# Expert weights in a mixture of experts: four gates, four ups, four downs per group, the four experts side by side

## The chip, the cores and the metric

The kernel runs on one core of a Trainium2 chip. The metric is the device time of one execution in microseconds (us); the kernel before has a median of 1077.59 us over three runs (1072.44 to 1079.12).

A core has a tensor engine (PE; its weight loads are shown as PEld), a vector engine (DVE), a scalar engine (ACT), a pool engine (POOL) and a sync engine (SP), which here issues nearly all transfers from DRAM.

## The reference

The program is a net of two blocks on 256 tokens of 1024 channels. The part that matters here is the mixture of experts at the end of the first block, with 32 experts of width 256 and two experts per token:

```python
def hier_moe(xn, w_group, b_group, w_router, b_router, w_gate, w_up, w_down):
    ...
    def per_sequence(args):
        xs, cw = args
        hg = jnp.einsum('sd,edf->sef', xs, w_gate)
        hu = jnp.einsum('sd,edf->sef', xs, w_up)
        act = jax.nn.silu(hg) * hu * cw[..., None]
        return jnp.einsum('sef,efd->sd', act, w_down)
```

The gate and up matrices of an expert are 1024 x 256, its down matrix is 256 x 1024, all float32: 1.05 MB each, 96 of them, 100.7 MB in all. The mixers, the attention and the two dense blocks around it are not touched.

## The kernel before

**Slots.** `route` gives each expert 32 slots for tokens. The experts are taken in eight groups g of four; `gather(S, g)` (line 1613) brings the tokens of a group's 4 x 32 slots, channels on partitions, into the tile `xg`, by 32 products into `pxg` and eight evacuations. An expert's 32 slots are one quarter of the array's 128 columns and one quarter of the partitions of the product's bank. If an expert has more than 32 tokens, `overflow` (line 1661) computes all; it stands behind a branch (line 1667) that all engines take ahead of group 2, and it does not run with these inputs.

**Products.** `gate_up(g, eps, p)` (line 1793) takes a list of expert pairs. For the gates, then for the ups, it goes over eight pieces j of the channels and, inside, over the experts of the list; each product has 32 slot columns as weights and 256 weight columns of the expert streaming, and goes to the expert's quarter of the bank `pgu`. For group 0 both pairs are in the list; from group 1 on `gate_up` is called once for each pair. `down(g, ...)` (line 1811) transposes the activations (`paT`, copied to `aT`), and multiplies them with the four down matrices: expert outermost, then the column half c, then the row half k, 512 columns each, into the two banks `pyd`. Each bank is scaled (`mg`, DVE), split in two parts (`mh` on ACT, `ml` on DVE), and eight products (`pacc`) add it to the token rows. In the main loop `down(g - 1)` stands between the two pairs of `gate_up(g)`. A float32 product is two records in the trace.

**Loads.** `moe_order` (line 1724) is the order of the 96 loads: gate, up, gate, up of a group's first pair, then the four downs of the group before, then the second pair. `moe_loads` gives each load a tile: one of the eight slots `w` (2048 columns, a ring in which load n waits for the readers of load n - 8), or, for the first 28 loads alone, idle work tiles `we` too. `moe_done` says that a weight is read, and announces the next loads. The loads for the attention behind the experts (`attn_w_in`, line 718) and for its modulation (`ada_w`, line 442) come in the same ring and on the same queue of SP, behind the last down.

**Order.** Each engine works its instructions off in a fixed order, laid out ahead of time; an instruction that waits holds up all that stand behind it on its engine.

Of the kernel before, what the change touches and what calls it, by code (L numbers as in the profile page):

```python
# [17 lines left out]
PSUM = bass.MemoryType.PSUM  # L18

T = 256  # L20
# [69 lines left out]
def shape_constants():  # L90
    """Tables that follow from the shapes alone, packed along the free axis."""
# [29 lines left out]
    # those of the first mixer, and two that are used once  # L121
# [15 lines left out]
    # mean over the last w tokens, less the token: columns t for rows s  # L137
# [15 lines left out]
class Net:  # L153
# [19 lines left out]
    # now: the tensor engine's time so far, by a coarse count of its columns and of the waits that fill() is told;  # L173
    # loaded: when the last load ends.  They only choose the order in which independent work is issued.
# [7 lines left out]
    def later(self, name, gen, lane=0):  # L182
        """lane 0: products; lane 1: products with one column, at the pace of their loads."""
        self.lanes[lane].append((name, gen))
# [15 lines left out]
    def fill(self, gap):  # L200
        """Queued work for a wait of that many microseconds."""
# [14 lines left out]
    def warm(self, n, after=None):  # L216
        """Products that nobody reads, for a wait of the tensor engine: its clock is halved after idle windows.
        They start when the columns `after` are there."""
# [8 lines left out]
    def more(self, n):  # L227
        """n steps of the second lane"""
        for _ in range(n):
            if self.lanes[1]:  # L230
                self.step(1)

    def need(self, *names):
        """Queued work up to the end of the named pieces."""
        for n in names:
            lane = next((i for i in range(2) if any(m == n for m, _ in self.lanes[i])), None)
            while n not in self.done:
                self.step(lane)

    def behind(self, *ins):  # L240
        """what is traced inside is issued behind these instructions on their engines"""
# [24 lines left out]
    def t4(self, name, dt=F32):  # L266
        """[128, 1024] work tile."""
# [14 lines left out]
    def used(self, waits=True):  # L282
        """the last slot is read by now"""
# [4 lines left out]
    def split(self, w, perm=None):  # L288
        """float32 [128, 1024] as a sum of two float32r parts; perm reorders the columns on the way."""
# [82 lines left out]
    def small_loads(self):  # L372
        """a few small loads behind a large one"""
# [22 lines left out]
    def rsqrt(self, out, v):  # L396
        """out = v ** -0.5 for a few columns, on the Pool engine."""
        return self.nc.gpsimd.tensor_tensor(out, v, self.mhalf.to_broadcast(list(v.shape)), op=ALU.pow)  # L398

    def head_rsqrt(self, sq, prep, between=None):  # L400
        """sq [128 (2 heads), 4 pairs, 256]: (prep(sum over a head))**-0.5 on every partition of the head;
        yields (bank, psum [128, 512])."""
# [11 lines left out]
    def tok_bcast(self, v, width, between=None):  # L414
        """v [128 tokens, (a, h)] -> per pair of 128-row groups, psum [128, 2, 256] with v[t, h]**-0.5 on width rows."""
# [21 lines left out]
    def ada_load(self, srcs, k):  # L437
        """rows 8 * p + k of the pieces, 2048 columns."""
# [7 lines left out]
    def ada_steps(self, which, srcs, rows, name, out, rowwise=False):  # L446
        """silu(c) @ W + b for four pieces of 512 columns: [128, 16], column j*4+q is channel chunk q of piece j;
        rows: where the biases of the first and of the second two pieces are."""
# [14 lines left out]
    def ada_half(self, half, m):  # L463
        """the first shift and scale for half of the channels: columns 4 * half.. and 8 + 4 * half.. of m."""
# [29 lines left out]
    def ada_cols(self, p, rows, name, out, rowwise=False):  # L494
        """out["m"]: channels 128 * column + partition; out["rows"]: channels 8 * partition + column"""
# [24 lines left out]
    def vector_sum(self, which, srcs):  # L520
        """silu(c) @ W for 2048 columns, on the vector engine: psum, 512 columns on each quarter of the partitions."""
# [19 lines left out]
    def ada_vector(self, which, srcs, rows, name, out):  # L541
        """as ada_steps, on the vector engine."""
# [3 lines left out]
    def gate_rows(self, l, out):  # L546
        """the gates of layer l of block 2 as rows in DRAM"""
# [23 lines left out]
    def rows_of(self, m, name):  # L571
        """m [128, 8 channel chunks] as rows on all partitions: [128, 1024]."""
# [16 lines left out]
    def combine(self, m, wname, w0, name):  # L589
        """per-channel scale w * (1 + scale); the shift is m[:, 0:8]."""  # L590
# [6 lines left out]
    def ss(self):  # L597
        """sums of squares [128 tokens, 3 parts of the channels, 2]"""
        return self.mpool.tile([128, 3, 2], F32, name="ss", tag="ss")

    def squares(self, ss, a, c, x, junk=None, first=True):
        """ss[:, c, a] = sum of squares of x [128, n]; the first half's is turned into its part of the mean."""
# [33 lines left out]
    def turn(self, xn, parts=1):  # L636
        """tokens [128, D] x 2 -> four banks [128 channels, 2 chunks x 256 tokens]."""
# [9 lines left out]
    def modulate(self, banks, scale, shift, fb=0):  # L647
        """normed rows in the channel layout, modulated: [128, 4 chunks x 256] x 2, with two float32r parts."""
# [57 lines left out]
    # Weights come as a stream of pieces in the order in which they are announced: each piece is split one ahead  # L706
    # of its use, over the borders between products too.
    def cols(self, W, c0, n, perm=None, kcs=range(8)):
        """announces columns c0..c0+n of W [1024, *] (n = 512 or 256), rows of the chunks kcs."""
# [1909 lines left out]
```

## Time and profile before

| what | us |
|---|---|
| median of three runs (lowest, highest) | 1077.59 (1072.44, 1079.12) |
| profiled execution, span from first to last instruction | 1071.7 |
| PE busy in it | 1018.5 (95%) |
| products `pgu` of the experts, first to last start | 293.2 to 535.2 |
| products `pyd`, last start | 548.7 |
| transfers, mean over the span | 265 GB/s |

The span is cut by the page into 40 slices of 26.8 us; the experts' products fill slices 11 to 20 (from 0, both included). In a row of the windows view the columns are the stretch, its length, the busy time of PE, PEld, DVE, ACT and POOL with the number of records, the granted clock of PE as a share of full speed, the busy share of the transfer engines, and GB/s. A busy PE is not a PE at its peak: records overlap, and four that run at the same time on four quarters of the array count as one busy stretch.

### The profile page before, as it was taken

Reading aid. Unit: us, or ns where it says so; the run is one execution under the profiler, and the core shown is the slowest. Engines: PE = TensorE matmul, PEld = TensorE weight load, DVE = VectorE, ACT = ScalarE, POOL = GpSimd, SP = SyncE. Lnnn points to the kernel's source line nnn. Section 1 sums busy time; section 2 is a strip of 40 time slices with the busy share of each in tenths; the row PEclk is TensorE's granted clock in tenths of the full one; section 3 lists DMA queues with packets and bytes.
Section 4 is the critical chain, followed back from the end, with each engine's and each line's share of the span. In section 5 each row is a group of like instructions: output and inputs, shape, how many; then the busy total and the mean of one; then the engine's idle time right before and its main releaser. Section 6 shows DMA issues by size and latency. Waiting matters only on the chain.

```text
span 1071.7 us, 18282 instructions
## 1 busy us (share of the span) xinstructions
PE 1018.5 (95%) x7681; PEld 771.9 (72%) x7681; DVE 558.5 (52%) x939; ACT 419.8 (39%) x685; POOL 40.7 (4%) x55
## 2 busy tenths in 40 slices
PE   5899999989998999999979999999999999999996
PEld 2587776776764544455338688999889889999995
DVE  1485645666612212102145746897878775544446
ACT  2363223252411111011036655655554557454453
POOL 1020000010100000000000001010000000000000
PEclk9999999997999999999999999999999999999999
DMA  8998856997786799989876732499998954555501
GB/s 270 312 323 328 300 198 237 364 353 266 270 343 237 272 370 392 369 340 399 343 276 209 263 114 101 156 352 373 359 331 342 322 190 158 165 195 191 196 1 40
DMA packets 88635, 284.53 MB, mean 265 GB/s; under 512 B 10526, under 2 KB 13907, under 8 KB 76519
## 3 DMA queue, kind: packets, MB, share of 16 engines
q1 hardware_dynamic: 86794, 280.31, 71.0%
q0 software_dynamic: 800, 1.57, 0.6%
q8 instruction: 61, 1.00, 0.4%
q10 hardware_dynamic: 956, 1.47, 0.4%
q14 instruction: 24, 0.19, 0.0%
HBM read 282.25 MB, written 1.07 MB: 264 GB/s over the span
## 4 chain that ended last, share of the span: by engine, by line
PE 62%; DVE 3%; ACT 1%; issue 1%; POOL 0%; POOLq 0%
PE pB L180 21%; PE pm L180 16%; PE pgu L180 8%; PE pyd L180 6%; PE pxg L180 2%; PE pacc L180 2%; PE po L180 2%; PE pgv L180 1%; PE pada L454 1%; PE pss L180 1%; PE pso L180 1%; DVE x L1428 0%; POOL rstd L398 0%; PE ppl L180 0%; DVE wl L294 0%
## 5 line engine op out<-in xcount | busy, mean ns | idle before, releaser
L294 DVE TENSOR_TENSOR wl<-w,wh 128x1024 fp32r<-128x1024 f32 x186 | 226.1, 1222 | 124.4 <-ACT wh L293 119.3
L293 ACT CAST wh<-w 128x1024 fp32r<-128x1024 f32 x186 | 194.0, 1049 | 208.2 <-PE pB L180 102.7
L180 PE MATMUL pB<-hh,wh 128*128 128x256 f32 x800 | 218.7, 289 | 2.3 <-ACT wh L293 1.5
L180 PE MATMUL pB<-hh,wl 128*128 128x256 f32 x800 | 215.3, 285 | 0.8 <-DVE wl L294 0.8
L180 PE MATMUL pB<-hl,wh 128*128 128x256 f32 x800 | 214.1, 284 | 0.8 <-DVE hl L654 0.7
L180 PEld LDWEIGHTS pB<-hh,wh 128*128 128x128 f32 x800 | 148.6, 191 | 18.2 <-issue 11.1
L180 PEld LDWEIGHTS pB<-hh,wl 128*128 128x128 f32 x800 | 147.9, 192 | 4.3 <-issue 2.3
L180 PEld LDWEIGHTS pB<-hl,wh 128*128 128x128 f32 x800 | 148.2, 192 | 1.5 <-DVE hl L654 1.2
L180 PE MATMUL pgu<-w,xg 128*32 128x256 f32 x864 | 105.6, 380 | 1.6 <-ACTq L1667 1.6
L180 PE MATMUL pm<-wh,fh 128*128 128x512 f32 (+1 forms) x262 | 101.3, 388 | 0.0
L180 PE MATMUL pm<-wl,fh 128*128 128x512 f32 (+1 forms) x262 | 100.9, 386 | 0.0
L180 PE MATMUL pm<-wh,fl 128*128 128x512 f32 (+1 forms) x262 | 100.7, 385 | 0.0
L180 PEld LDWEIGHTS pgu<-w,xg 128*32 128x32 f32 x864 | 51.9, 110 | 48.7 <-issue 7.6
L1829 DVE SCALAR_TENSOR_TENSOR mg<-pyd,slotw,g_f 128x512 f32<-128x512 f32 x16 | 12.0, 751 | 129.7 <-PE pyd L180 110.4
L534 DVE SCALAR_TENSOR_TENSOR w<-w,csil 128x1024 f32<-128x1024 f32 x56 | 70.3, 1277 | 4.3 <-DMA w<-in_ada_w_dram 4.3
L180 PE MATMUL pyd<-w,aT 128*32 128x512 f32 x208 | 62.2, 595 | 0.9 <-ACT aT L1816 0.9
L180 PEld LDWEIGHTS pm<-wh,fh 128*128 128x128 f32 x262 | 49.2, 188 | 12.2 <-ACT fsq L2231 2.5
L180 PEld LDWEIGHTS pm<-wh,fl 128*128 128x128 f32 x262 | 49.3, 188 | 9.8
L180 PEld LDWEIGHTS pm<-wl,fh 128*128 128x128 f32 x262 | 49.3, 188 | 9.6 <-DVE wl L294 0.3
L180 PEld LDWEIGHTS pyd<-w,aT 128*32 128x32 f32 x208 | 16.5, 110 | 38.6 <-issue 37.2
L1830 ACT CAST mh<-mg 128x512 fp32r<-128x512 f32 x16 | 9.7, 618 | 81.3 <-DVE mg L1829 81.3
L454 PE MATMUL pada<-w,csil 128*32 128x512 f32 x256 | 39.3, 603 | 0.0
(554 smaller groups left out, 1332.3 us busy)
## 6 DMA issues: line engine op xcount, KB each, us to landing
w<-in_mlp_w_dram SPq DMA_DIRECT2D x64, 1024.0 KB
w<-in_ada_w_dram SPq DMA_DIRECT2D x40, 1024.0 KB
w<-in_ada_w_dram SPq DMA_DIRECT2D x64, 512.0 KB
w<-in_moe_w_gate_dram SPq DMA_DIRECT2D x27, 1024.0 KB
w<-in_moe_w_up_dram SPq DMA_DIRECT2D x27, 1024.0 KB
w<-in_moe_w_down_dram SPq DMA_DIRECT2D x25, 1024.0 KB
w<-in_w_in_dram SPq DMA_DIRECT2D x12, 1024.0 KB
w<-in_attn_w_in_dram SPq DMA_DIRECT2D x9, 1024.0 KB
```

The source lines that it names most:

```text
L180: self.nc.tensor.matmul(out, lhsT, rhs, **kw)
L293: nc.scalar.copy(h, w)
L294: self.split_ins = nc.vector.tensor_sub(l, w, h)
L454: nc.tensor.matmul(acc[32 * j:32 * j + 32, :], self.csil[:, which, k:k + 1].to_broadcast([128, 32]), w[:, j * 512:(j + 1) * 512], start=(k ...
L534: nc.vector.scalar_tensor_tensor(acc[:, s], w[:, s], ck, acc[:, s], op0=ALU.mult, op1=ALU.add)
L1829: nc.vector.scalar_tensor_tensor(yg[:, s], py[c], cwg, gate[:, s], op0=ALU.mult, op1=ALU.mult)
L1830: self.down_ins = [nc.scalar.copy(yh[:, s], yg[:, s]), nc.vector.tensor_sub(yl[:, s], yg[:, s], yh[:, s])]
```

## The change

The order of the loads is by kind: the four gates of a group, its four ups, its four downs. `gate_up` is called once for each group, with four experts inside each j, and `down` of a group follows its own `gate_up`, the gather of the next group and the slot weights, and no longer stands inside the next group. In `down` the expert is the innermost loop, inside c and k. `moe_done` of the gates, and then of the ups, names four weights in place of two. The residual's products stand ahead of the last `down`. Comments and docstrings are gone, which moves line numbers by 5 to 8. Nothing is computed otherwise.

```diff
     def moe_order(self):
-        for g in range(9):
-            for ep in range(2):
-                if g < 8:
-                    for e in (4 * g + 2 * ep, 4 * g + 2 * ep + 1):
-                        yield "gate", e
-                        yield "up", e
-                if g > 0 and ep == 0:
-                    for e in range(4 * g - 4, 4 * g):
-                        yield "down", e
+        for g in range(8):
+            for kind in ("gate", "up", "down"):
+                for e in range(4 * g, 4 * g + 4):
+                    yield kind, e
...
-        def gate_up(g, eps, p):
-            es = [e for ep in eps for e in (2 * ep, 2 * ep + 1)]
+        def gate_up(g, p):
             for m, kind in enumerate(("gate", "up")):
                 for j in range(8):
-                    for e in es:
+                    for e in range(4):
...
-                self.moe_done(*((kind, 4 * g + e) for e in es))
+                self.moe_done(*((kind, 4 * g + e) for e in range(4)))
...
-            for e, k, c in ((e, k, c) for e in range(4) for c in range(2) for k in range(2)):
+            for c, k, e in ((c, k, e) for c in range(2) for k in range(2) for e in range(4)):
...
             p = self.ps("pgu")
+            gate_up(g, p)
             if g == 0:
-                gate_up(0, (0, 1), p)
                 self.overflow_flag(S)
                 gate = self.ada_gate(S["gate"], 1, "g_f")
-            else:
-                gate_up(g, (0,), p)
-                down(g - 1, *prev)
-                gate_up(g, (1,), p)
+            t = act(p)
             self.slot_weights(S, g)
-            prev = act(p), S["ot"], S["cwg"]
+            ot, cwg = S["ot"], S["cwg"]
             if g < 7:
                 self.gather(S, g + 1)
...
-        residual()
-        down(7, *prev)
+            if g == 7:
+                residual()
+            down(g, t, ot, cwg)
         return acc, fw, fw2
```

On PE, one group in the middle of the stage, before: the second pair's `pgu` and the `paT` of a group, then the first pair of the next group, then the downs, and the next pair. `pcw` are the slot weights, `pxg` the next gather.

```order
L180 MATMUL pgu<-w,xg 32x256 x32
L1814 MATMUL paT<-cs,actm 128x128 x2
L180 MATMUL pgu<-w,xg 32x256 x31
L180 MATMUL pyd<-w,aT 32x512 x16
L1642 MATMUL pcw<-cs,oh 128x128 x2
L180 MATMUL pcw<-cw,oh 128x32 x2
L180 MATMUL pacc<-mh,slotT 128x512 x2
L180 MATMUL pxg<-oh,xp 128x128 x2
```

The same place now:

```order
L180 MATMUL pgu<-w,xg 32x256 x61
L1809 MATMUL paT<-cs,actm 128x128 x2
L180 MATMUL pyd<-w,aT 32x512 x16
L180 MATMUL pacc<-mh,slotT 128x512 x2
L180 MATMUL pgu<-w,xg 32x256
L180 MATMUL pacc<-ml,slotT 128x512 x2
L180 MATMUL pacc<-mh,slotT 128x512
L180 MATMUL pacc<-ml,slotT 128x512
L180 MATMUL pacc<-mh,slotT 128x512
L180 MATMUL pacc<-ml,slotT 128x512
L1642 MATMUL pcw<-cs,oh 128x128 x2
```

The 61 rows in one piece are gates and ups of all four experts, and the downs follow the transposes at once; one product of the next group's gates has moved up between the `pacc`.

On SP, the last loads of the experts and the first behind them, before:

```order
L1763 DMA w<-in_moe_w_gate_dram 128x2048
L1763 DMA w<-in_moe_w_up_dram 128x2048
L1761 DMA w<-in_moe_w_down_dram 128x2x1024 x4
L1763 DMA w<-in_moe_w_gate_dram 128x2048
L1763 DMA w<-in_moe_w_up_dram 128x2048
L1763 DMA w<-in_moe_w_gate_dram 128x2048
L1763 DMA w<-in_moe_w_up_dram 128x2048
L1761 DMA w<-in_moe_w_down_dram 128x2x1024 x3
L1758 DMA w<-in_moe_w_down_dram 128x2x512 x2
L718 DMA w<-in_attn_w_in_dram 128x8x256
```

And now:

```order
L1758 DMA w<-in_moe_w_gate_dram 128x2048 x4
L1758 DMA w<-in_moe_w_up_dram 128x2048 x4
L1756 DMA w<-in_moe_w_down_dram 128x2x1024 x3
L1753 DMA w<-in_moe_w_down_dram 128x2x512 x2
L718 DMA w<-in_attn_w_in_dram 128x8x256
```

In the ring of eight, a down now takes the slot of a gate of its own group, the next group's gates take those of the ups, and its ups those of the downs. The loads behind the last down, and all other queues, have kept their order.

## Rows read from the trace of the kernel before

**Rows 1.** Windows view, three stretches of the experts' stage, with its column line.

```profile
core 0: us, PE busy (x) PEld busy (x) DVE busy (x) ACT busy (x) POOL busy (x), PEclk, DMA share, GB/s
406.50:440.00 33.50, 32.03 (x216) 16.01 (x214) 5.49 (x13) 4.93 (x11) 0.00 (x0) 1.00 0.92 371
440.00:474.20 34.20, 32.03 (x228) 17.44 (x226) 5.49 (x13) 5.98 (x12) 0.00 (x0) 1.00 0.89 356
505.60:549.50 43.90, 41.80 (x193) 14.93 (x190) 5.29 (x12) 2.98 (x6) 0.00 (x0) 1.00 0.94 368
```

**Rows 2.** Windows view, two stretches of ten us inside the same stage.

```profile
440.00:450.00 10.00, 10.00 (x64) 3.80 (x61) 0.00 (x0) 0.00 (x0) 0.00 (x0) 1.00 1.02 412
480.00:490.00 10.00, 10.00 (x46) 4.24 (x42) 3.12 (x5) 1.41 (x3) 0.00 (x0) 1.00 1.01 422
```

**Rows 3.** Windows view: all of group 0's gate_up; one pair; one group's downs.

```profile
293.20:300.30 7.10, 7.10 (x130) 4.13 (x130) 0.00 (x0) 2.79 (x5) 0.00 (x0) 1.00 0.57 205
307.20:314.20 7.00, 7.00 (x66) 3.63 (x65) 0.00 (x0) 1.50 (x4) 0.00 (x0) 1.00 1.01 414
410.30:418.80 8.50, 8.50 (x35) 2.33 (x32) 0.75 (x1) 0.62 (x1) 0.00 (x0) 1.00 1.02 425
```

**Rows 4.** Timeline of PE, a group's pair and downs: start, length, line, products.

```profile
403.45 6.88 PE L180 MATMUL pgu<-w,xg 128*32 128x256 f32 x61
...
410.38 8.41 PE L180 MATMUL pyd<-w,aT 128*32 128x512 f32 x31
```

**Rows 5.** Timeline of SP's queue: first gate loads of groups 6 and 7, later loads.

```profile
440.16 0.34 SPq L1763 DMA_DIRECT2D w<-in_moe_w_gate_dram  x1
...
474.33 0.34 SPq L1763 DMA_DIRECT2D w<-in_moe_w_gate_dram  x1
...
531.77 4.39 SPq L718 DMA_DIRECT2D w<-in_attn_w_in_dram  x4
541.61 6.29 SPq L442 DMA_DIRECT2D w<-in_ada_w_dram  x3
```

**Rows 6.** Timeline of PE, from group 0 to the branch ahead of group 2.

```profile
302.12 0.38 PE L1642 MATMUL pcw<-cs,oh 128*128 128x128 f32 x2
...
303.39 3.84 PE L180 MATMUL pxg<-oh,xp 128*128 128x128 f32 x32 [0.52 <-DVE oh L1617]
...
339.20 0.40 PE L180 MATMUL pgu<-w,xg 128*32 128x256 f32 x1 [1.59 <-ACTq L1667]
```

**Rows 7.** Timeline of ACT, the gathered tokens' evacuation in group 0.

```profile
307.26 1.50 ACT L1635 ACTIVATE xg<-pxg,fr,sc_f 128x128 f32<-128x128 f32 x4 [3.01 <-PE pxg L180]
```

**Rows 8.** Chain of work that ended last, in order of time, the last group.

```profile
537.09 0.42 PE paT L1814 x2
537.54 0.38 ACT aT L1816
537.96 3.66 PE pyd L180 x13
...
547.64 0.76 DVE mg L1829
548.42 0.63 ACT mh L1830
549.08 0.69 DVE ml L1830
549.77 0.67 DVE mg L1829
```

**Rows 9.** Instructions of the tile `pyd`: ns shortest, median, longest, starts.

```profile
L180 PE MATMUL pyd<-w,aT x208: 592/593/618, 324.1 to 548.7; 128*32 128x512 f32 x104
```

**Rows 10.** Line 1928 (POOL's two loads of 512 KB), time to landing.

```profile
DMA to landing us min/median/max: 4.1/5.8/7.5
```

**Rows 11.** Windows view, stretches of two us ahead of the experts' stage.

```profile
262.00:264.00 2.00, 1.61 (x4) 1.17 (x4) 2.00 (x3) 0.96 (x2) 0.00 (x0) 0.50 0.12 47
264.00:266.00 2.00, 2.00 (x6) 0.19 (x4) 1.84 (x4) 0.00 (x0) 0.00 (x0) 0.50 0.60 156
266.00:268.00 2.00, 2.00 (x10) 1.44 (x9) 0.00 (x0) 0.00 (x0) 0.00 (x0) 0.93 1.02 397
```

**Rows 12.** Windows view, a stretch of ten us behind the experts' stage.

```profile
560.00:570.00 10.00, 9.65 (x72) 7.46 (x72) 9.08 (x16) 7.63 (x15) 0.00 (x0) 1.00 0.34 115
```

More of the change, by code (lines that the diff above doesn't have):

```diff
@@ L1847, in residual @@
                             start=False, stop=False)
-        prev = None
         for g in range(8):
```

## Prediction

> **What bounds the kernel now.** I went first to the windows view of the experts' stage (293 to 549 us of the span). In its later groups PE is busy for 32.0 of 33.5 and of 34.2 us, and the transfers run at a share of 0.89 to 0.94 with 356 to 371 GB/s [rows 1]. Both look full, so the question is which of the two has air in it.
>
> PE has. Group 0 is the one group whose gates and ups already have all four experts side by side: 130 records in 7.1 us [rows 3]. One pair alone, 66 records and so half the work, takes 7.0 us [rows 3]. A column quarter of the array thus takes its own share of the time, the quarters run together, and a pair leaves half of the array idle. The downs are worse: with the expert outermost, neighbouring products share a quarter, and 32 records take 8.5 us [rows 3, 4]. Each streams twice the columns of a gate record; at the pace of group 0 (7.1 us for 32 steps of four records, 0.22 us a step), 8 steps of 0.44 us would be 3.5 us.
>
> The transfers have little. Where nothing holds them up they move 412 to 422 GB/s at a busy share of 1.01 and more [rows 2]. Over a whole group the rate is lower, because SP waits for PE to read slots. With 12 loads of 1.0486 MB per group, 417 GB/s means 2.51 us a load and 30.2 us a group, where the loads of group 7 begin 34.2 us behind those of group 6 [rows 5].
>
> So the change takes about half of PE's product time out of the stage, and the stage then runs into the transfers. The gain is what lies between 256 us and the time of the bytes, plus what the start and the end cost.
>
> **The change, step by step.** The sum goes in the profiled execution (span 1071.7 us).
>
> *Start, PE still the bound.* Up to the end of the gather for group 1 (303.39 + 3.84 = 307.2 us) nothing moves [rows 6]. Then, instead of group 1's first pair, the downs of group 0: 0.87 us from `paT` to `pyd` [rows 8], 3.5 us of products, and some 3.0 us through `mg` 0.76, `mh` 0.63, `ml` 0.69 [rows 8] and the last `pacc`: 314.6. Gate and up of group 1, 7.1 us [rows 3]: 321.7. Slot weights and gather, from 302.12 to 307.2 in group 0 and so 5.1 us [rows 6]: 326.8. ACT evacuates the gathered tokens ahead of `aT`, 1.5 us [rows 7], plus 0.87: 329.2. Downs 3.5 and the way to the last `pacc` 3.0: 335.7. Branch, 1.6 us of wait [rows 6]: 337.3. Before, PE passes the branch at 339.2 [rows 6] with the downs of group 1 still to do. Gate and up of group 2, 7.1: 344.4.
>
> In that time the loads are not late: 20 of 96 were issued before 293 us, the next eight take 20 us from the first release at 297 us, the ups of group 2 get their slots by 321.7, and its downs by 332.7 and the branch. They are through by about 341. The first loads of group 3 take the slots of group 2's ups, so they start when those are read: 344.4.
>
> *Middle, the transfers the bound.* From there on only the ring of eight is left. A down needs the slot of a gate of its own group, which is read while the ups come in; the next gates need the ups' slots, read while the downs come in. PE's work per group is 7.1 + 3.5 + 5.1 + 3.0 + 1.5 (activation) + 0.9 = 21.1 us against 30.2, and each piece (3.5 to 8 us) fits into the 10 us in which four loads come. So PE's work is hidden behind the transfers; if that cover went, a group would cost its excess over 30.2. The residual, 7 us in group 7, lies in such a wait too. Sixty loads from 344.4 take 60 x 2.51 = 150.8 us. Of the two bias tables that POOL fetches behind the branch I charge one, 512 KB, 1.3 us; the other falls into the pause before 344.4. Last byte: 496.5 us.
>
> *End.* What is late next is the last down. I have no landing time for SP's loads; POOL's of 512 KB land in 4.1 us at the shortest [rows 10], less 1.3 us of bytes 2.8 us. That is my upper bound, zero the lower; I take 2.8 since the start at 344.4 also holds an issue: 499.3. The last expert's load comes in two column halves, and c is now outermost, so its first half is done 1.3 us sooner. Left are four steps for each half. At full clock both are through at 501.6, at half clock (3.6 us each) at 505.2.
>
> PE will have waited some ten us with single products in between. This trace shows 2.4 GHz through the whole stage (1.00 in every window), but the clock at 0.50, that is 1.2 GHz, at 262 to 266 us, where only four to six products stand in two us; it rose again in the dense stretch from 266 us [rows 11]. I take 505.2. Before, the last `pyd` ends at 548.7 + 0.6 = 549.3 [rows 9]. That is 44.1 us. Behind it lie the first `pacc` and the norm; with the clock still rising I give back 1 us, between 0 and 3.
>
> *Behind the stage.* The attention's first four loads were issued at 531.8 and three more for the modulation at 541.6, ahead of the stage's end [rows 5]. Now they queue behind the last down, and the latter wait for its slots, which all come free at the end and not expert by expert. So the seven come about 10 us later against the end of the stage. The first of them, which the attention needs first, still lands with it; the rest has the stretch at a share of 0.34 as cover [rows 12]. I charge nothing; if that cover failed, up to 5 us.
>
> Sum: 1071.7 - 44.1 + 1.0 = 1028.6 us of span. The three runs lie 0.7 to 7.4 us above this span, their median 5.9, so **1034 us** beside 1077.6.
>
> **Rules that speak against it.** In the Trainium skill, "DMA: Bandwidth & Descriptors", the section "Where 436 GB/s comes from" says that from DRAM to the core's memory about 358 GB/s per core is the limit. By that a load would take 2.93 us, and the estimate would be 25 us later, some 1059. The trace does not agree: 412 to 422 GB/s over ten us [rows 2]. "TensorE: Matmul & The Clock Gate", section "HAM oscillation — how this bites in real kernels", says that products that wait for transfers in every round find the clock throttled each time; that is the last rival below, and this stage, kept busy so far, cannot show it.
>
> **The rivals.**
>
> *Downs not four wide.* No row shows 512-column products on four quarters in turn. If they stay at 8.5 us, that is 5 us more for groups 0, 1 and 2 each before the ring runs evenly, 5 at the end, and a pause of some 1 us where the ups wait for the downs' slots in the other four: 24 us, 1058. For it: 1.6 quarters at a time is what the trace has for 512 columns. Against it: the order, not the width, explains that, and `pgu` shows full overlap.
>
> *Slower transfers.* If the long windows, 356 to 371 GB/s [rows 1], are the true long-run rate and not gaps made by PE, say 365, a load costs 2.87 us, and sixty cost 22 us more: 1056. Against it, a share of only 0.89 to 0.94 in the same rows.
>
> *Handovers.* If a release reaches SP late or PE's pieces run past 8 us, because they start at 1.2 GHz, each of the three handovers in a group leaves a pause. At 1 us each over four groups: 12 us, 1046.
>
> *No gain.* The stage stays as it is, because its time is already that of the bytes, 1072 to 1079. That needs the rate of rows 1 and a late start together.
>
> *Slower than before: half clock all through.* If the clock stays at 1.2 GHz in the whole stage, the products double: 14.2 + 7.0 + 10.2 + 3.0 + 1.5 + 0.9 = 36.8 us a group, 294 for eight instead of 256, and the result is some 1115 us. It ends up slower from the point at which a group takes over 32 us, that is with two thirds of this work at half clock. For it: the dip of rows 11. Against it: PE would then have no waits left, and in the dense stretch of rows 11 the clock came back.
>
> **How the numbers follow.** The main case gets 0.72. From its bounds (landing 0 to 2.8, end at full or half clock, give-back 0 to 3, cover behind the stage 0 to 5, offset of the runs 0.7 to 7.4) it spans 1024 to 1042. Handovers 0.09, downs not four wide 0.06, slower transfers 0.06, no gain 0.04, slower 0.03. The range goes from 1024 up to 1052, which takes in the handovers and leaves out the other rivals and a little of the main case's edge. A measurement of this kernel can tell about 1% from no change. All cases but the last two are faster by more than that: 0.93 faster, 0.04 within 1%, 0.03 slower.
>
> **What would show it.** The gate and up of each group in one dense piece of about 7 us where the weights are there, or in two pieces of 3.5 us behind waits for transfers. The downs at 3.5 us when their loads are in; at 8 us the first rival is right. From group 3 on, first loads of groups some 30 us apart and 410 GB/s and more in every window of ten us up to about 495 us; steadily lower at a share of 1.0 is the second rival, gaps in the share the third. PE waiting for transfers where it waited for nothing. The clock at 0.5 in pieces of the stage, but back within each product piece; a PE full at half clock is the last rival. The last `pyd` near 505 us instead of 549, and the attention behind it as long as before. I am wrong if the loads of group 3 start much after 345 us, or if the stretch behind the stage grows by what the stage lost.

## The result and the profile after

The changed kernel takes 1039.7 us (median of four runs, 1036.57 to 1042.31) where the kernel before took 1078.36 us in the same session (four runs, 1072.44 to 1080.31): a ratio of 0.966, 95% interval 0.962 to 0.970. The forecast was 1034 us in a range of 1024 to 1052. The profiled execution has a span of 1034.8 us, the one of before 1071.7: 36.9 us less, where the sum of the prediction had 43.1.

| what (profiled execution, us) | before | forecast | after |
|---|---|---|---|
| gates of group 0 begin | 293.2 | 293.2 | 293.8 |
| first load of group 3 issued | | 344.4 | 347.0 |
| second half of the last down landed | | 499.3 | 510.2 |
| last `pyd` ends | 549.3 | 505.2 | 512.4 |
| from there to the end of the span | 522.4 | 523.4 | 522.4 |
| span | 1071.7 | 1028.6 | 1034.8 |
| median of the runs | 1078.36 | 1034 | 1039.7 |

All of the gain lies inside the experts' stage. The forecast's error lies there too: the stage ends 7.2 us later than predicted, and behind it 1 us that the forecast had given back was not needed. The stretch behind the stage is as long as before to a tenth of a us.

**The products are four wide.** Timeline of PE in the changed kernel (start, length, line, product, tile written and read, records; in brackets the wait ahead of it and what ended it), group 0's downs, a wait inside the gates of group 2, group 2's downs, and the downs of group 3:

```profile
308.55 3.64 PE L180 MATMUL pyd<-we,aT 128*32 128x512 f32 x32 [0.46 <-ACT aT L1811]
...
343.30 0.40 PE L180 MATMUL pgu<-we,xg 128*32 128x256 f32 x1 [1.57 <-issue]
...
355.19 3.64 PE L180 MATMUL pyd<-w,aT 128*32 128x512 f32 x32 [1.64 <-ACT aT L1811]
...
379.18 7.20 PE L180 MATMUL pyd<-w,aT 128*32 128x512 f32 x32 [0.46 <-ACT aT L1811]
```

32 records of the downs take 3.64 us, where 32 took 8.5 [rows 3, 4]. The last row is the same piece at half clock, 7.20 us.

**PE now waits for weights.** The chain that ended last by engine, first before, then after, and the groups of instructions of the experts' products (busy us and mean ns, then the idle time just before and what ended it), from the page:

```profile
PE 62%; DVE 3%; ACT 1%; issue 1%; POOL 0%; POOLq 0%
PE 56%; DMA 5%; DVE 3%; issue 1%; ACT 1%; POOL 0%; SPq 0%; POOLq 0%; ACTq 0%
```

```profile
L180 PE MATMUL pgu<-w,xg 128*32 128x256 f32 x848 | 61.5, 390 | 5.9 <-DMA w<-in_moe_w_up_dram 5.9
```

Transfers now stand in the chain with 5%; before it had none. In the windows view of the middle, ten us each (columns as in [rows 1]; the last three are PE's granted clock, the transfers' share and GB/s):

```profile
370.00:380.00 10.00, 7.29 (x73) 3.31 (x74) 0.84 (x2) 3.32 (x8) 0.00 (x0) 0.97 1.02 407
380.00:390.00 10.00, 9.76 (x46) 3.78 (x42) 2.79 (x4) 1.24 (x2) 0.00 (x0) 0.86 1.02 422
...
400.00:410.00 10.00, 6.65 (x94) 2.93 (x82) 0.84 (x2) 0.76 (x2) 0.00 (x0) 1.00 0.85 327
...
430.00:440.00 10.00, 7.62 (x126) 4.11 (x124) 0.84 (x2) 2.03 (x3) 0.00 (x0) 1.00 0.79 320
...
490.00:500.00 10.00, 9.23 (x115) 4.07 (x117) 0.00 (x0) 0.00 (x0) 0.00 (x0) 1.00 0.85 329
```

Most windows show 417 to 423 GB/s at a share of 1.01 and more, the pace that the forecast took from [rows 2] for all of them. Three do not: at 400, 433 and 495 us the transfers pause. Each lacks some 90 GB/s over ten us, that is 2.2 us of transfer time; with the smaller dents in the windows from 350 (367 GB/s) and 360 us (399) it is some 8 us.

What holds them up stands in two places. SP's queue (start, length until the last of the four is issued):

```profile
346.99 2.09 SPq L1758 DMA_DIRECT2D w<-in_moe_w_gate_dram  x4
358.84 2.02 SPq L1758 DMA_DIRECT2D w<-in_moe_w_up_dram  x4
...
385.56 1.75 SPq L1758 DMA_DIRECT2D w<-in_moe_w_up_dram  x4
401.15 2.15 SPq L1756 DMA_DIRECT2D w<-in_moe_w_down_dram  x4
```

and PE ahead of the issues at 401.15 and at 496.03:

```profile
392.07 3.17 PE L180 MATMUL pxg<-oh,xp 128*128 128x128 f32 x26
...
395.72 2.24 PE L180 MATMUL pbf<-bflip,cs 128*128 128x512 f32 x4
397.89 3.66 PE L180 MATMUL pgu<-w,xg 128*32 128x256 f32 x64
...
484.96 3.68 PE L180 MATMUL pacc<-xp,diag 128*128 128x512 f32 x4
...
489.12 3.70 PE L180 MATMUL pacc<-xp,diag 128*128 128x512 f32 x4
492.75 4.07 PE L180 MATMUL pgu<-w,xg 128*32 128x256 f32 x66
```

Four downs cannot be loaded before the four gates of their group are read. The gates of group 4 are read from 397.89 on, though their loads were issued at 376.42 and the ups behind them at 385.56: on PE they stand behind the gather (`pxg`) and the bias rows (`pbf`). The gates of group 5 stand behind the gather and the norm rows (`pgate`, up to 430.4 us), those of group 7 behind the residual's eight products, 7.4 us. The smaller pause near 359 us is another one: the ups of group 3 are issued at 358.84, when the downs of group 2, whose slots they take, have been read.

The end of the stage, on PE and in its weight loads (PEld):

```profile
508.81 3.62 PE L180 MATMUL pyd<-w,aT 128*32 128x512 f32 x20 [0.67 <-DMA w<-in_moe_w_down_dram]
```

```profile
510.20 0.16 PEld L180 LDWEIGHTS pyd<-w,aT 128*32 128x32 f32 x7 [0.40 <-DMA w<-in_moe_w_down_dram]
```

The last expert's down comes in two column halves. The first one releases the products at 508.81, the second is waited for until 510.20.

### The profile page after: what moved, and what is told of

Same layout as the page of the kernel before. It is cut to its first block, busy times and chain, and to the rows that moved or that the text cites. A ratio compares the mean times of both kernels' runs of the same rounds, so it can differ in the third digit from the quotient of the medians.

```text
span 1034.8 us, 18299 instructions
## 1 busy us (share of the span) xinstructions
PE 959.8 (93%) x7681; PEld 744.6 (72%) x7681; DVE 559.2 (54%) x939; ACT 419.8 (41%) x685; POOL 40.7 (4%) x55
## 3 DMA queue, kind: packets, MB, share of 16 engines
q0 software_dynamic: 800, 1.57, 0.6%
## 4 chain that ended last, share of the span: by engine, by line
PE 56%; DMA 5%; DVE 3%; issue 1%; ACT 1%; POOL 0%; SPq 0%; POOLq 0%; ACTq 0%
PE pB L180 22%; PE pm L180 16%; DMA w<-in_moe_w_down_dram 5%; PE pgu L180 3%; PE pyd L180 2%; PE pxg L180 2%; PE po L180 2%; PE pacc L180 2%; PE pgv L180 1%; PE pada L454 1%; PE pss L180 1%; PE pso L180 1%; DVE x L1428 0%; POOL rstd L398 0%; PE ppl L180 0%
## 5 line engine op out<-in xcount | busy, mean ns | idle before, releaser
L180 PE MATMUL pgu<-w,xg 128*32 128x256 f32 x848 | 61.5, 390 | 5.9 <-DMA w<-in_moe_w_up_dram 5.9
L180 PE MATMUL pyd<-w,aT 128*32 128x512 f32 x216 | 45.7, 653 | 9.2 <-ACT aT L1811 5.6
L180 PEld LDWEIGHTS pgu<-w,xg 128*32 128x32 f32 x848 | 30.2, 112 | 33.4 <-DMA w<-in_moe_w_up_dram 8.3
L1802 DVE TENSOR_TENSOR actm<-sgm,pgu 128x256 f32<-128x256 f32 x8 | 3.3, 418 | 80.9 <-ACT sgm L1801 80.9
L180 PEld LDWEIGHTS pyd<-w,aT 128*32 128x32 f32 x216 | 11.3, 115 | 38.4 <-issue 19.7
```

Source lines behind the costliest of these rows:

```text
L180: self.nc.tensor.matmul(out, lhsT, rhs, **kw)
L1802: nc.vector.tensor_mul(t, sg, p[:, 0:256])
```

## The experiments

**The two halves of the change, each alone.** First the changed kernel with the downs in the old order:

```diff
-            for c, k, e in ((c, k, e) for c in range(2) for k in range(2) for e in range(4)):
+            for e, k, c in ((e, k, c) for e in range(4) for c in range(2) for k in range(2)):
```

> The changed kernel with one part undone: in down the expert is the outermost loop again. Theory (start bound by PE, middle bound by the bytes): the downs of groups 0 and 1 cost 5 us more each (8.5 instead of 3.5), those of group 2 some 3 to 5; from group 3 on each expert's downs can run as soon as its own load lands, 2.1 us of products per 2.5 us of load, so nothing is added there and at the end; 1039.7 + 10 to 15 = 1050 to 1055. Rival A (PE's products set the pace all through): 5 us in each of eight groups, 40 us, about 1080. Rival B (the order of the downs does nothing, all of the gain is from gates and ups): 1040.

Measured: 1060.16 us, ratio 0.989 (0.984 to 0.993), span 1054.9. PE's timeline and SP's queue in this run:

```profile
308.52 8.86 PE L180 MATMUL pyd<-we,aT 128*32 128x512 f32 x32 [0.46 <-ACT aT L1811]
```

```profile
355.14 2.07 SPq L1758 DMA_DIRECT2D w<-in_moe_w_gate_dram  x4
```

The piece is 8.86 us long instead of 3.64, group 3's loads begin 8.1 us later, and the last `pyd` starts at 530.4 instead of 511.8. This is close to the time that the prediction's first rival ("downs not four wide", 1058) had worked out. The theory written for the run, 1050 to 1055, was too low. It let the downs from group 3 on run beside the loads of their group, but those of group 3 stand behind them in one piece of 8.86 us; the gates of group 4 are read later for it, and the transfers pause:

```profile
391.66 8.86 PE L180 MATMUL pyd<-w,aT 128*32 128x512 f32 x32 [0.46 <-ACT aT L1811]
```

```profile
410.00:420.00 10.00, 9.76 (x129) 4.69 (x128) 0.00 (x0) 2.88 (x7) 0.00 (x0) 1.00 0.34 121
```

Then the kernel before with nothing but the downs in the new order:

```diff
-            for e, k, c in ((e, k, c) for e in range(4) for c in range(2) for k in range(2)):
+            for c, k, e in ((c, k, e) for c in range(2) for k in range(2) for e in range(4)):
```

> The kernel before with one part of the change alone: in down the expert is the innermost loop, loads and pairs as before. Theory (PE sets the pace before): groups 0 to 2 gain 5 us each, groups 3 to 6 come down from 33.5 to some 31 us each, where the transfers take over at 30.2, and the last downs gain up to 5: 25 to 30 us, 1048 to 1053. Rival A (PE all through, no floor by the bytes): 40 us, 1038. Rival B (downs hidden already): under 5 us, 1073 or more.

Measured: 1047.99 us, ratio 0.977 (0.973 to 0.981), span 1040.9. Windows view:

```profile
366.00:400.00 34.00, 32.06 (x253) 17.31 (x250) 6.17 (x14) 5.42 (x12) 0.00 (x0) 1.00 1.02 417
...
480.00:506.00 26.00, 25.38 (x136) 9.81 (x134) 3.26 (x8) 1.61 (x3) 0.00 (x0) 1.00 1.02 411
```

In spans: before 1071.7, downs alone 1040.9, gates and ups with the order of the loads alone 1054.9, both 1034.8. So 30.8 of the 36.9 us come with one line, the order inside `down`, and 6.1 more with all the rest. These are single executions, those of the three kernels with changes each the shortest of its runs. By the medians of the runs (ratios 0.977, 0.989 and 0.966) the one line gives 2.3 of 3.4%, two thirds. In spans the two halves do not add up (30.8 and 16.8), in medians they do (2.3 and 1.1%), so these runs leave open how far one half takes from the other. In this second kernel the transfers run from 366 to 506 us at 411 to 417 GB/s without a pause, although pairs still leave half of the array idle.

**Are the bytes the bound?** Two kernels load half of every expert weight and use that half twice:

```diff
-                    nc.sync.dma_start(w, src[:, 0])
+                    nc.sync.dma_start(w[:, 0:1024], src[:, 0, 0:1024])
...
-        return w[half]
+        return w[0]
```

> The changed kernel with every expert load cut to its first half (512 KB); the products are all there, but those of the second half read the first half again, so the computation is changed. Theory (bytes are the bound from group 3 on): a group then costs PE's own 21 to 23 us instead of 31 to 33, the last down ends at about 455 to 465 us instead of 512, and the time is 985 to 995. Rival A (the waits on the handovers of slots or the half clock of PE set the pace, not the bytes): 1030 to 1040.

> The kernel before with every expert load cut to its first half in the same way, all products kept (the second half's products read the first half, so the computation is changed). Theory (before, PE is the bound and the transfers hide behind it): no more than 5 us gained, 1070 to 1078. Rival (the stage was bound by its bytes before, too): a gain of 20 us or more, 1055 or less.

Measured: with the change 1003.96 us (span 1002.3, 32.5 us less than with all bytes), without it 1064.17 (span 1062.4, 9.3 us less). Each is one run. The changed kernel misses the 985 to 995 of its theory, since the last `pyd` ends at 478.4 us and not at 455 to 465, but is far below the rival's 1030. One group of it takes 23.3 to 26.3 us, from first load to first load, of the one before 31.9. Windows view, first the changed kernel with half of the bytes, then the one before:

```profile
346.80:445.00 98.20, 89.23 (x873) 50.21 (x872) 22.47 (x55) 19.27 (x44) 0.00 (x0) 0.98 0.75 258
```

```profile
375.20:470.90 95.70, 95.27 (x651) 51.19 (x648) 16.26 (x39) 15.21 (x34) 0.00 (x0) 1.00 0.60 198
```

Before, PE is busy for 95.27 of 95.70 us even with half of the bytes: PE was the bound, though the bytes cost it some 9 us in this run (the runs of the kernel before spread over 8), more than the theory had and less than the rival. Now the bytes are. The pace with half of the bytes, 23.3 to 26.3 us a group with PE's waits for other engines in it, is slower than the 21.1 us that the prediction had summed, but still well below 30.

**Taking PE's small work away from the gates.** If the pauses come from gates queued behind the gather, the remedy is to put the gather elsewhere. First try: slot weights, gather, bias rows and the residual behind the last up of the group instead of ahead of its gates:

```diff
-            self.slot_weights(S, g)
-            ...
+            with self.behind(*([last] if g > 1 else [])):
+                self.slot_weights(S, g)
+                ...
```

The changed kernel itself was run again beside it, in five runs.

> The changed kernel itself once more, as the measure for the runs beside it: 1035 to 1043.

> The changed kernel with the small products of a group (slot weights, gather for the next group, the bias and norm rows) set behind the last up of the group from group 2 on, and the residual split in two behind the downs of groups 5 and 6. Theory (the transfers stand still for some 2.5 us at 400, 433 and 495 us since the gates of groups 4, 5 and 7, whose slots the downs need, stand behind these products on PE): those three pauses go, 7 us, so 1033 beside 1040, span 1027 to 1028. Rival (the pauses are the time that a release takes to reach a transfer, or the half clock of PE): they stay, under 2 us gained; moved into the waits for the downs they may also delay these, then up to 3 us are lost.

> The kernel of the run before it with four more loads that may go to idle work tiles (32 instead of 28), which takes three ups of group 2 out of the ring, so three of group 3's gates need the slots of group 1's downs, not those of group 2's ups. Theory (from the first loads of group 3 on every us at the start is one at the end, as the bytes are the bound): group 3 starts at 335 to 340 us instead of 347 and the end comes 5 us earlier than in the run before it: span 1021 to 1024. Rival (the start is bound by PE's products and an earlier load only waits): no gain.

Measured: the changed kernel 1041.05 us (ratio 0.966, 0.963 to 0.970), the first try 1051.84 (0.979, 0.976 to 0.982), with four more loads in work tiles 1046.59 (0.975, 0.970 to 0.979). The theory fell. In the first try (PE, then a window):

```profile
375.98 6.29 PE L180 MATMUL pgu<-w,xg 128*32 128x256 f32 x58 [1.90 <-DMA w<-in_moe_w_up_dram]
...
384.49 5.44 PE L180 MATMUL pxg<-oh,xp 128*128 128x128 f32 x32 [1.48 <-DVE oh L1617]
```

```profile
380.00:390.00 10.00, 8.52 (x65) 7.02 (x57) 2.63 (x9) 0.79 (x3) 0.00 (x0) 0.76 1.02 416
390.00:400.00 10.00, 9.16 (x50) 2.98 (x48) 2.80 (x4) 3.94 (x9) 0.00 (x0) 1.00 0.65 265
```

PE waits for the ups with nothing else to do, three waits in a row of 1.7 to 1.9 us. The clock is then at 0.76 over ten us, the ups take 6.29 us, the gather 5.44 instead of 3.84, the downs come later, and now the next ups wait for the downs' slots: the pause has moved to 394 us and is longer (265 GB/s). With four more loads in work tiles the loads of group 3 begin at 334.40 us, but the ups of group 3 are still issued at 359.34, when the downs of group 2 are read:

```profile
334.40 13.82 SPq L1758 DMA_DIRECT2D w<-in_moe_w_gate_dram  x4
359.34 1.98 SPq L1758 DMA_DIRECT2D w<-in_moe_w_up_dram  x4
```

**Single products that keep PE busy at the end.** The kernel has a `warm` call inside the last downs. Without it (`W8 = 0`):

> The changed kernel without the two products that nobody reads ahead of the last downs. Theory (they, with the four downs ahead of them, are what brought the clock back for the last downs, which then take 3.6 us): at half clock the last 20 records take up to 7.2 us, the last one starts 2 to 3.6 us later against the landing of the last load, time 1042 to 1044. Rival (the clock is at 2.4 GHz there anyway): 1040 and 3.6 us.

```profile
515.73 3.62 PE L180 MATMUL pyd<-w,aT 128*32 128x512 f32 x20 [1.14 <-DMA w<-in_moe_w_down_dram]
```

20 records of the last downs take 3.62 us, as they do with it (3.62 at 508.81): not a sign of half clock, and no help to the question of why the tail ran at full clock. The time of this one run, 1048.03 us, is above the changed kernel's; its span is 11.4 us longer, of which 2.4 lie ahead of the stage, 4.5 inside it and 4.5 behind it, where there is a stretch at a clock of 0.71 and 0.78 (610 to 630 us). One run does not show that the missing products did that.

**Filling the wait for the ups.** The same small work behind the last *gate*, so that PE does it while the ups come in, from group 1 on:

```diff
-        def gate_up(g, p):
+        def gate_up(g, p, between=None):
...
                 self.moe_done(*((kind, 4 * g + e) for e in range(4)))
+                if m == 0 and between:
+                    with self.behind(last):
+                        between()
...
-            gate_up(g, p)
+            gate_up(g, p, (lambda: small(g)) if g >= G8 else None)
```

> The changed kernel, but from group 1 on the slot weights, the gather of the next group, the first bias rows and norm rows, and the residual's products (one half each in groups 6 and 7) stand on PE between the last gate and the ups of a group, in place of between the ups and the downs. Theory, that the pauses of the transfers near 400, 433 and 495 us (2.5 us each and slower approach to them, together about 7 to 10 us) come from gates that are queued on PE behind this work: the gates of groups 4, 5 and 7 are now read as soon as the last of them has landed, the downs' loads are not held, and the downs need only the activation behind the ups. PE does the small work while the ups come in, so its waits do not grow and the clock stays. Some 7 to 8 us less than the changed kernel: 1031 to 1034 us, a ratio to the kernel before of 0.957 to 0.960, and 415 GB/s and more in every window of ten us from 365 to 500 us. Rival, as with the gather behind the ups: the pauses come back at another place, since the ups are now read up to 8 us later than they land and the next gates' loads wait for their slots; then 1040 us or more, ratio 0.965 or more, with pauses at the first loads of a group.

> The same kernel as the other one of this call, with four more loads (the four ups' or downs' places in turn) in idle work tiles at the start, 32 in place of 28. Theory: the first load that needs a slot of the ring read comes earlier, the loads of group 3 begin at 335 to 340 us in place of 347, and as the transfers are the bound from there on, up to 5 us more are saved if the third up of that group does not wait again for the downs of group 2 to be read: 1028 to 1033 us, ratio 0.954 to 0.959. Rival: a pause at 354 to 361 us gives it back, as it did with the gather behind the ups, and the time is that of the other kernel of this call.

Measured: 1038.0 us (ratio 0.966, 0.963 to 0.969) and 1036.99 (0.964, 0.961 to 0.967). No gain that these runs can tell from the changed kernel, and more than the 1031 to 1034 and 1028 to 1033 of the theories, yet the middle of the first did what its theory said. Windows view and SP's queue of the first:

```profile
350.00:360.00 10.00, 8.08 (x97) 3.82 (x96) 2.05 (x5) 2.28 (x7) 0.00 (x0) 1.00 0.72 281
...
400.00:410.00 10.00, 10.00 (x86) 6.35 (x82) 1.94 (x7) 3.05 (x7) 0.00 (x0) 1.00 1.01 408
...
430.00:440.00 10.00, 9.85 (x101) 7.55 (x94) 1.94 (x7) 3.15 (x8) 0.00 (x0) 1.00 1.02 415
...
490.00:500.00 10.00, 8.50 (x66) 3.11 (x58) 0.17 (x2) 0.37 (x1) 0.00 (x0) 0.88 1.01 413
```

```profile
353.63 2.03 SPq L1759 DMA_DIRECT2D w<-in_moe_w_gate_dram  x4
```

All three pauses are gone, 408 to 415 GB/s where there were 320 to 329. From the first load of group 3 to the end of the last `pyd` it takes 158.0 us instead of 165.4. But the loads of group 3 begin 6.6 us later, of which 1.8 are a later start of the stage (295.6 us): the ups of group 2, whose slots they take, are now read behind the gather. The same edit that frees the gates delays the ups. In the second kernel the loads of group 3 begin at 337.14 us, but the ups behind them wait until 363.49, and the transfers fall to 280 and 209 GB/s from 350 to 370 us, as its rival had it:

```profile
363.49 1.97 SPq L1759 DMA_DIRECT2D w<-in_moe_w_up_dram  x4
```

So the old order in groups 1 and 2, the new one from group 3 on (`G8 = 3`); and, beside it, 32 loads instead of 28 that may use work tiles, with the gather of group 3 behind the downs of group 2:

> As the run that put the small work (slot weights, gather, bias and norm rows, halves of the residual) behind the gates, but only from group 3 on; groups 1 and 2 are as in the changed kernel. That run had no pause from 360 to 510 us, but its loads of group 3 began at 353.6 us instead of 347.0, because the ups of group 2 were read behind the gather, 354 instead of 347, and their slots are what those loads wait for. Theory: with the old order in groups 1 and 2 the loads of group 3 begin at 347 again, the pause near 358.5 us (the ups of group 3 wait for the downs of group 2) stays at about 2 us, and from there on the transfers run without a pause: the last product of the stage ends near 506 us, a span of about 1029 us, 1029 to 1033 us as median, ratio 0.955 to 0.960. Rival: the time of this kernel is not set by where these loads begin; then the median stays at 1037 to 1041 us, ratio 0.963 to 0.967, and what the middle gains is lost elsewhere again.

> The other kernel of this call, and in addition 32 loads with idle work tiles in place of 28, and in group 2 the gather of group 3 behind the downs instead of ahead of them. Both aim at the transfers between 334 and 360 us alone: with 32 the four gates of group 3 are issued from 334 us on and the next loads wait for the downs of group 2, which are then read 5 us earlier, at about 353 instead of 359 us. Theory: the ups of group 3 are issued near 353.5 us, a pause of 2 to 4 us stays ahead of them, the rest follows without a pause: 5 us less than the other kernel, 1024 to 1028 us, ratio 0.950 to 0.956. Rival: 32 loads in work tiles or PE's wait for the activation cost what the earlier downs give, then it is within 2 us of the other kernel.

Measured: 1039.5 us (ratio 0.966, 0.963 to 0.968) and 1032.99 (0.961, 0.957 to 0.965). The first kernel's stage came out as forecast, its time did not: it is the rival's (1037 to 1041). SP's queue and PE:

```profile
345.39 2.06 SPq L1759 DMA_DIRECT2D w<-in_moe_w_gate_dram  x4
357.25 1.97 SPq L1759 DMA_DIRECT2D w<-in_moe_w_up_dram  x4
```

```profile
500.41 4.98 PE L181 MATMUL pyd<-w,aT 128*32 128x512 f32 x24 [0.33 <-DMA w<-in_moe_w_down_dram]
```

```profile
503.20 0.16 PEld L181 LDWEIGHTS pyd<-w,aT 128*32 128x32 f32 x7 [0.43 <-DMA w<-in_moe_w_down_dram]
```

The stage ends at 505.4 us (506 expected) instead of 512.4; it began 1.8 us earlier than in the changed kernel, so 5.2 us are its own. The clock still dips in its middle (0.83 from 390 to 400 us) while the transfers hold 415 GB/s, so half clock alone makes no pause:

```profile
390.00:400.00 10.00, 8.94 (x87) 5.78 (x88) 0.84 (x4) 0.37 (x1) 0.00 (x0) 0.83 1.00 415
```

The span is 1036.9 all the same: the stretch behind the stage takes 531.5 us instead of 522.4. There, in the attention, with PE busy throughout:

```profile
600.00:610.00 10.00, 10.00 (x49) 9.54 (x49) 1.11 (x2) 1.64 (x2) 0.00 (x0) 0.50 0.00 0
610.00:620.00 10.00, 10.00 (x46) 9.78 (x46) 3.08 (x6) 3.79 (x5) 2.90 (x2) 0.51 0.30 106
```

```profile
592.37 1.15 PE L181 MATMUL pds<-gv,gkT 64*64 64x128 f32 x24
...
618.89 0.63 PE L181 MATMUL po<-wh,yh 128*128 128x512 f32 x1
```

The clock is at half for 20 us. From `pds` to the first `po` it takes 26.5 us, where the changed kernel takes 17.8:

```profile
599.42 1.15 PE L180 MATMUL pds<-gv,gkT 64*64 64x128 f32 x24
...
617.22 0.40 PE L180 MATMUL po<-wh,yh 128*128 128x512 f32 x1
```

That is 8.7 of the 9.1 us. The last kernel, 5 us ahead of the other at its first ups of group 3 after allowing for its later start, loses that lead later in the middle (369 GB/s from 360 to 370 us, 385 from 400 to 410, 363 from 460 to 470), and its stage ends at 505.6 us, no earlier. Of its stage's theory only the first step held:

```profile
333.76 13.71 SPq L1759 DMA_DIRECT2D w<-in_moe_w_gate_dram  x4
353.45 1.91 SPq L1759 DMA_DIRECT2D w<-in_moe_w_up_dram  x4
```

In its profiled execution `pds` to `po` takes 19.3 us, and that, not the stage, is why its span is 6.8 us shorter than the other kernel's. What slows the transfers in those three windows is open. It has the lowest median of this study, above the 1024 to 1028 of its theory; two of its six runs took 1039 us and more, and its interval overlaps that of the changed kernel.

**What the runs' times follow.** Span and mean granted clock of the six runs of that kernel, ordered:

| span, us | 1028.1 | 1028.8 | 1030.1 | 1032.4 | 1037.5 | 1038.1 |
|---|---|---|---|---|---|---|
| mean clock | 0.985 | 0.984 | 0.982 | 0.979 | 0.974 | 0.973 |

The kernel before with only the downs reordered shows the same: 1040.9, 1043.8, 1048.5, 1050.9 us at 0.991, 0.988, 0.984, 0.983. In others the order is looser (with `G8 = 3` 1038.3 us at 0.976, but 1039.3 at 0.981).

Two traces of the changed kernel itself show where such a difference can lie. In the runs beside the first try its profiled execution has a span of 1044.9 us at a mean clock of 0.975, where the one above has 1034.8 at 0.987. Of the 10.1 us, 4.5 lie ahead of the stage, 4.8 inside it (3.7 of them before the first load of group 3) and 0.8 behind it. One of the stretches at a lower clock:

```profile
350.00:360.00 10.00, 8.61 (x93) 5.79 (x86) 1.52 (x6) 0.76 (x2) 0.00 (x0) 0.83 0.64 244
```

So two executions of one kernel differ by 4.8 us in the length of the stage, about as much as several kernels above do. The stretch from the first load of group 3 to the end of the last `pyd` is steadier: 165.4 and 166.6 us in these two, 158.0 and 160.0 in the kernels with the small work behind the gates from group 1 and from group 3 on. What those gain in the middle is therefore more than this spread.

Medians of the mean clock: before 0.991, changed kernel 0.983, small work behind the gates 0.981, the first try (gather behind the ups) 0.968. 0.8% of 1036 us is 8 us: the estimate of how much the change at most gives back through the clock, if all of PE's time at half clock stood on the path. Some of it falls into waits, where it can cost nothing.

## Why the prediction was right, and where it was off

*What bounds the kernel.* Right. Halving the bytes takes 9.3 us off the kernel before and 32.5 off the changed one, in one run each; PE was the bound, the transfers are now.

*Downs at 3.5 us.* Right, 3.64 where the loads were in and the clock was full (groups 0 and 2). The rival (8.5 us, 1058 us) did not come; forced by the old order it measured 1060.16.

*Start, 344.4 us for the first load of group 3.* 347.0. The gates of group 2 begin at 338.07 us, 0.8 behind the sum's 337.3: group 0 began 0.6 us later and the wait for DVE's `oh` ahead of the gather of group 2 is 1.48 us where the forecast took the 0.5 of group 0 [rows 6], but the branch costs a wait of 0.52 us and not 1.6. The other 1.8 us arise inside group 2's gates and ups, which had 7.1 us in the sum: PE stands still for 1.57 us ahead of the row at 343.30. Nothing that the profile shows ended that wait; its cause is open.

*The middle, 60 loads at 2.51 us and nothing else.* Here the prediction failed: "each piece (3.5 to 8 us) fits into the 10 us in which four loads come. So PE's work is hidden", and "the residual, 7 us in group 7, lies in such a wait too". From the first load of group 3 to the landing of the last half the sum had 154.9 us, measured were 163.2 (346.99 to 510.20). Each piece does fit, but pieces stand one behind the other in a fixed order: downs, `pacc`, slot weights, gather, bias rows or residual, and only then the gates, whose slots the downs' loads want. Three pauses of some 2.2 us and the smaller dents near 359 us make up the difference of 8.3. The kernel with the small work behind the gates from group 3 on takes 157.8 us for the same stretch (345.39 to 503.20), 5.4 less, and keeps the pause ahead of the ups of group 3 (357.25): the pace was right to within some 3 us, the term for handovers was missing. The "handovers" rival named the symptom, a pause at each handover (12 us, 1046), with other causes (late releases, half clock); it came at some 8 us, and for the greater part because of the order on PE. How much of the first pause is due to the piece of 7.20 us that stands ahead of it was not tested.

*The end at half clock, 5.9 us from landing to the last product.* 2.2 us (510.20 to 512.43): the last 20 records ran at full clock (3.62 us at 508.81), the case that the sum had at 2.3 us and did not take. The clock did dip in the middle, as the piece of 7.20 us at 379.18 and the window at 0.86 show, but not there. In the second trace of this kernel the first eight of the last downs do run at half clock (3.83 us) and the other 24 at full clock (3.68). This wrong step hid 3.7 us of the other error, which is luck. Together: 2.6 + 8.3 - 3.7 = 7.2 us.

*Behind the stage.* "I charge nothing" for the attention's later loads was right, 522.4 us on both sides; the 1 us given back to the clock was not needed in this execution. In other kernels of this study the same stretch took up to 531.5 us, so that it came out at the same tenth is partly luck of the executions.

*The offset of the runs.* The median lies 4.9 us above the profiled span, 5.4 were taken. The prediction had no reason for this spread; the table above shows that the mean clock goes with it, not what sets the clock.

*Slower transfers, no gain, half clock all through.* None came. The Trainium skill, "DMA: Bandwidth & Descriptors", "Where 436 GB/s comes from", would cap a core at about 358 GB/s; over the 140 us from 366 to 506 the kernel with only the downs reordered moved 411 to 417. The Trainium skill, "TensorE: Matmul & The Clock Gate", "HAM oscillation — how this bites in real kernels", which has products between waits for transfers at a lower clock, agrees with the trace in kind: half clock shows in four places of the middle of the changed kernel and in the first try far more. While the transfers are the bound it can cost little, as the window at 0.83 with 415 GB/s above shows; that it costs where it delays the reading of slots is a reading of the first try, which no run tests by itself.

## What to carry to other kernels

When several small products share the array by columns, write the loop so that neighbouring products go to different quarters: the same 32 records took 3.64 us instead of 8.86, and this one line held two thirds (medians) to five sixths (spans) of the gain. Once transfers are the bound, look at which instruction frees the slot that the next load wants, and at everything that stands ahead of it on its engine; it is not enough that each piece of work fits into the time of the loads. Moving that work helps only if the slots it now delays are not wanted first, and a gain of some us in a stage must be looked for again at the end of the span: in the execution traced here it was spent in a stretch at half clock that no wait explains.

## What the hardware showed that was not expected

The clock fell to half behind the stage in a stretch in which PE was busy for 10.00 of 10.00 us on both sides, some 94 us after the end of the stage, for 20 us in one kernel (0.50 and 0.51 in two windows) and not at all in the profiled executions of before and of the changed kernel (both of them) at the same instructions. In six more kernels it fell there for a part of the time (windows at 0.71 to 0.92). What stands there are products that stream 64 columns each (`pgo`, `pgi`) between ones of 256. Why it fell in some and not in others is open, and with it, in part, why the kernels whose middle has no pauses are hardly faster.
